# RWKV preparation: shifted mixing read from PSUM, three banks for the in-projection, low parts of its weights on the vector engine

## The chip, the cores and the metric

The kernel runs on one core of a Trainium2 chip. The time is the device time of the whole program in microseconds (us); before the change it is 1434.59, the median of 3 runs (1434.33 to 1435.47).

The engines are named as the profile names them: PE multiplies matrices (PEld loads its stationary operand), DVE is the vector engine, ACT the scalar engine, POOL the GpSimd engine, SP only issues DMAs. Each takes its instructions in the order in which the compiler's scheduler has put them. SBUF is the on-chip memory. PSUM, where PE writes its results, has eight banks of 128 partitions x 512 float32 values.

## The reference, cut to what matters

Two layers over 256 latent and 256 context tokens of width 1024. The first mixes tokens with RWKV-7 heads and differential attention side by side, the second is a Mamba-2 mixer; each ends with an MLP. The change lies in the preparation of the RWKV heads:

```python
def centred_shift(p):
    prev = jnp.pad(p[:, :-1], ((0, 0), (1, 0), (0, 0)))
    nxt = jnp.pad(p[:, 1:], ((0, 0), (0, 1), (0, 0)))
    return 0.5 * (prev + nxt)

# rwkv_prepare: p is the first 1792 columns of h @ w_in, for latent and context tokens
    p = p + (centred_shift(p) - p) * mu
    r, k, v, wd, ad, gd = jnp.split(p, ...)
    kkf = hd(k * k_k)
    kk = kkf * lax.rsqrt(jnp.sum(kkf * kkf, axis=-1, keepdims=True) + 1e-12)
```

So every column of the projection becomes `(1 - mu) * p[t] + (mu / 2) * (p[t-1] + p[t+1])`, with zero beyond the ends of each of the two sequences.

## The kernel before, in words

Activations lie transposed, 128 channels on the partitions, 512 tokens (256 latent, 256 context) along the free dimension. To keep float32 accuracy with the faster matmul type, a matrix is split in a high part (rounded) and a low part (the rest), and a product is three matmuls: high by high, high by low, low by high.

The in-projection runs over tiles of 128 columns. `unit` (line 359) is one half of such a tile: four blocks of 128 rows, twelve matmuls 128x512 into one bank; `in_half` (line 367) calls it for both halves. The weights of a unit come through `w_ahead` (line 349): a DMA on SP's queue into `rw`, ACT's copy into the high part `rh` (line 355), and a subtraction into the low part `rl` (line 356) on the engine that `enqueue` (line 370) gave, POOL by default. All three rings have three buffers, and each unit that starts asks for the weights two units on. Fourteen tiles (28 units) belong to the RWKV preparation, twelve more to attention, whose projection follows and partly overlaps; the same rings later serve the out-projection.

`units` (line 660) is the backbone of the preparation: it projects a tile, and `shiftmix` (line 537) evacuates and mixes it. ACT copies the bank into a padded tile `pad` and writes the bank scaled by 1 - mu to `smq`; DVE adds the padded tile's two shifted views (`sms`) and combines both with mu / 2 into the result (`krv`, or once each `wda` and `sg`). After each step `units` runs small pieces of work from the list `after` (line 690): per pair of heads `kk_norm` (line 553: squares, a small matmul into `kkps`, a reciprocal square root of eleven DVE operations on eight columns, tiles `nw_x`, `nw_t`, `nw_y`, then a matmul `kkb` that spreads it and a DVE multiply `kk`), `v_tok`, and `stream` for context and latent tokens (line 582: decay matmuls `zp`, `ap`; DVE, ACT and POOL work on `lt`, `cs`, `e`; products AR and BK; matmuls `Lps`; a small matmul `bp` and the store `bond` of `bo` on SP's queue). One step of `ada`, the modulation vectors of the layer (matmuls `adaps`), is run per unit as well. After the last stream, the 64x64 triangular inverses (`rwkv_T`, line 441) start with 62 dependent DVE operations each, and attention's projections and softmax run beside them.

PSUM in this part: pool `mm` two banks (in-projection), `g` three (`kkps`, `kkb`, `vp`, `bp`, `gt`), `ch` three. The three stay open to the end of attention. The order on each engine is not that of the program text alone: a scheduler at compile time orders by priority and by when it estimates operands to be ready.

Of the kernel before, what the change touches and what calls it, by code (L numbers as in the profile page):

```python
# [7 lines left out]
F32 = mybir.dt.float32  # L8
F32R = mybir.dt.float32r
I32 = mybir.dt.int32  # L10
AF = mybir.ActivationFunctionType
# [4 lines left out]
ADD, SUB, MUL, MIN, MAX = ALU.add, ALU.subtract, ALU.mult, ALU.min, ALU.max  # L16

D = 1024
T = 256
NT = 512  # L20
# [31 lines left out]
def build(ctx: ExitStack, tc, xT, cT, pk_d, ct_d, ca_d, cs_d, lora_d, gup_d, cb_d, ada_w, adaT, w_in, w_out, w1, w2,  # L52
          s_in, s_dt, s_out, out, dbg=None, stop=None):
    nc = tc.nc
    act, dve, pool, pe = nc.scalar, nc.vector, nc.gpsimd, nc.tensor

    def dump(name, ap):
        if dbg is not None and name in dbg:
            nc.sync.dma_start(out=dbg[name], in_=ap)
# [4 lines left out]
    cm = ExitStack()  # L64
    mid = cm.enter_context(tc.tile_pool(name="mid", bufs=1, side="right"))
    dram = ctx.enter_context(tc.tile_pool(name="dram", bufs=1, space=DRAM))
    def ps_pools(stack, *bufs):
        for n, b in zip(("mm", "g", "ch"), bufs):
            PS[n] = stack.enter_context(tc.tile_pool(name=f"ps_{n}", bufs=b, space=PSUM, reuse_waits="tile"))

    PS = {}
# [5 lines left out]
    def tt(o, a, b, op):  # L77
        dve.tensor_tensor(o, a, b, op)  # L78

    def ts(o, a, s1, op0, s2=None, op1=None):  # L80
        if op1 is None:
            dve.tensor_scalar(o, a, s1, None, op0)
        else:
            dve.tensor_scalar(o, a, s1, s2, op0, op1)

    def stt(o, a, s, b, op0, op1):
        dve.scalar_tensor_tensor(o, a, s, b, op0, op1)  # L87

    def actf(o, i, f, scale=1.0, bias=0.0, **kw):
        act.activation(out=o, in_=i, func=f, scale=scale, bias=bias, **kw)  # L90

    def psm(shape, name="mm"):
        return PS["mm"].tile(shape, F32, name=name, tag="mm")

    def psg(shape, name="g"):
        return PS["g"].tile(shape, F32, name=name, tag="g")
# [52 lines left out]
    def kview(w):  # L149
        return w.rearrange("(p j) n -> p j n", j=8)  # L150
# [175 lines left out]
    E2 = [slice(0, 64), slice(64, 128)]  # L326
    Q = lambda d, b: slice(64 * d + 32 * b, 64 * d + 32 * b + 32)
    with ExitStack() as c1:
        ps_pools(c1, 2, 3, 3)
        reg = c1.enter_context(tc.tile_pool(name="reg", bufs=1))  # L330

        cr = reg.tile([128, NCT - 256], F32, name="cr")
# [8 lines left out]
        wv = kview(w_in)  # L341
# [25 lines left out]
        def in_half(ps, i):  # L367
            unit(ps, hh, hl, 4 * i, i == 0, i == 1)

        def enqueue(v, cols, ks=(0, 4), engs=(pool,)):  # L370
            todo.extend((v, c, k, engs[i % len(engs)]) for i, c in enumerate(cols) for k in ks)

        for k in (0, 4):
            enqueue(wv, [1536, 512], (k,))
        enqueue(wv, [0, 1024])
        for hp in range(1, 4):
            enqueue(wv, [512 + 128 * hp, 128 * hp, 1024 + 128 * hp])
        enqueue(wv, [1664])
        for hd in range(4):
            enqueue(wv, [1792 + 512 * i + 128 * hd for i in range(3)])  # L380

# [4 lines left out]
        with tc.tile_pool(name="x0", bufs=1) as xp:  # L386
# [3 lines left out]
            i = iter(range(16))  # L390
# [114 lines left out]
        with tc.tile_pool(name="prep", bufs=1) as pp:  # L505
            def ring(name, shape, bufs):
                return pp.tile(shape, F32, name=name, tag=name, bufs=bufs)
# [7 lines left out]
            mu1, muh = sm[:, 32:46], sm[:, 46:60]  # L515
# [7 lines left out]
            ts(rkh, PV("rk"), 0.5, MUL)  # L523
            wda = pp.tile([128, NT], F32, name="wda")
            sg = pp.tile([128, NT], F32, name="sg")
            pads = [pp.tile([128, 2, T + 2], F32, name=f"pad{i}") for i in range(2)]
            for p_ in pads:
                pool.memset(p_[:, :, 0:1], 0.0)
                pool.memset(p_[:, :, T + 1:T + 2], 0.0)
            e1s = [pp.tile([128, 2, 4, 66], F32, name=f"e1{i}") for i in range(2)]  # L530
            for e in e1s:
                e = e.rearrange("p d c t -> p (d c) t")
# [1 line left out]
                pool.memset(e[:, :, 65:66], 1.0)  # L534
            rot = [0]

            def shiftmix(n, o, ps=None):
                if ps is None:
                    ps = psm([128, NT], "inps")
                    in_half(ps, 0)  # L540
                    yield
                    in_half(ps, 1)
                pad = pads[rot[0] % 2]
                rot[0] += 1
                p3 = lambda a: a.rearrange("p (s t) -> p s t", s=2)
                actf(pad[:, :, 1:T + 1], p3(ps), AF.Copy)
                q = ring("smq", [128, NT], 2)
                s = ring("sms", [128, NT], 2)
                actf(q, ps, AF.Identity, scale=mu1[:, n:n + 1])
                tt(p3(s), pad[:, :, 0:T], pad[:, :, 2:T + 2], ADD)  # L550
                stt(o, s, muh[:, n:n + 1], q, MUL, ADD)

            def kk_norm(hp, k):

# [104 lines left out]

            def units():  # L660

                p2 = [psm([128, NT], "inps") for _ in range(2)]
                for i in range(2):
                    for ps in p2:
                        in_half(ps, i)
                    yield
                yield from shiftmix(12, wda, p2.pop(0))
                actf(wda[0:64], wda[0:64], AF.Tanh)
                yield
                for hp in range(4):  # L670
                    krvs.append([])
                    for sec in (1, 0, 2):
                        krvs[hp].append(ring("krv", [128, NT], 6))
                        yield from shiftmix(4 * sec + hp, krvs[hp][-1], p2.pop() if p2 else None)
                        yield
                yield from shiftmix(13, sg)
                actf(sg, sg, AF.Tanh, scale=0.5)
                ts(sg, sg, 0.5, MUL, 0.5, ADD)
                yield
                for _ in range(2):  # L680
                    early.append(psm([128, NT], "inps"))
                    for i in range(2):
                        in_half(early[-1], i)
                        yield
# [17 lines left out]
            with ExitStack():  # L702
                for u, _ in enumerate(units()):
                    for f in after.get(u, ()):
                        f()
                    if u > 1:
                        next(A, None)
                run((A, 1))
            dump("wda", wda)
            dump("sg", sg)  # L710

        at = c1.enter_context(tc.tile_pool(name="at", bufs=1, reuse_waits="tile"))

# [394 lines left out]


    ps_pools(ctx, 3, 2, 3)  # L1110
    wpool = ctx.enter_context(tc.tile_pool(name="w", bufs=2, reuse_waits="tile"))
    def gemm_first(pss, wts, rh, rl, n, lat_norm=None):
# [147 lines left out]
    with ExitStack() as c1:  # L1260
# [14 lines left out]
        def t1k(shape, name, **kw):  # L1275
            return sp.tile(shape, F32, name=name, tag="t1k", bufs=4)
# [5 lines left out]
        ps = done.pop(0)  # L1282
# [7 lines left out]
        f = [t1k([128, 4, 64], f"sf{i}") for i in range(4)]  # L1290
        tt(dts, pt, PV("dtb").unsqueeze(1).to_broadcast([128, 4, 64]), ADD)
        e, r, s2, p_ = f
# [18 lines left out]
        cp = psg([128, 4, 64], "cps")  # L1311
# [376 lines left out]
```

## Time and profile before

| | |
|---|---|
| median of 3 runs | 1434.59 us |
| the profiled execution | 1438.96 us, of which the span from first to last instruction is 1437.2 |
| busy share of the span | PE 94%, DVE 74%, ACT 44%, POOL 21% |
| granted PE clock, mean | 0.974 of full |

How to read it: "busy" is the time in which an engine had an instruction running. A row of a group names the line of the kernel, the engine and the operation, the output tile, an arrow and the inputs, the shape and the count; then busy us, mean ns of one, and the idle time just before them with what ended it. A row in order of time begins with start and duration in us; a bracket at its end is the idle time before it and who released it. The line can be that of a helper (L75 is every matmul, L78 every `tensor_tensor`, L84 and L82 `tensor_scalar`, L87 `scalar_tensor_tensor`, L90 every activation), so tiles tell more than lines. The chain of waits that ended last was followed back as far as 472 us only, so for the preparation, which lies before that, the stretches and the waits are read instead.

### The profile page before, as it was taken

The page shows a single profiled execution, that of the slowest core. Times are in us where ns is not written, and L with a number is a line of the kernel's source. Part 1 is how long each engine was busy: PE and PEld are TensorE (multiplying, and loading weights), DVE is VectorE, ACT ScalarE, POOL GpSimd, SP SyncE. Part 2 cuts the span into 40 slices and gives each one's busy share as a digit, 9 for nine tenths or more (in the row PEclk, how much of TensorE's full clock was granted, in tenths as well). Part 3 has the DMA queues.
Part 4 walks back from the last instruction along what each step waited for, and adds up shares of the span by engine and source line. Part 5 has one row for each costly group of instructions (what it writes and reads, how often), then busy time and mean ns, then how long its engine had stood idle before and what let it go on. Part 6 is the DMA issues. An engine that isn't in the chain of part 4 may idle for free.

```text
span 1437.2 us, 25996 instructions
## 1 busy us (share of the span) xinstructions
PE 1351.4 (94%) x10026; PEld 1139.1 (79%) x10026; DVE 1059.2 (74%) x2217; ACT 638.8 (44%) x1200; POOL 302.5 (21%) x228
## 2 busy tenths in 40 slices
PE   5899998899998799999999999999999989999997
PEld 2566666677877788888888897888888879999997
DVE  3778869864778898987667567697778784766665
ACT  2544444454543444224232243665555533455543
POOL 0355443111004300000000001233333335311110
PEclk9999999899999899999999999999999999999999
DMA  9455565234143556656667433655444323566653
GB/s 343 146 186 183 180 181 139 56 89 170 44 143 95 155 156 188 185 179 210 211 196 214 146 107 95 164 168 140 132 117 133 103 88 93 155 188 183 191 178 102
DMA packets 311324, 220.42 MB, mean 153 GB/s; under 512 B 30176, under 2 KB 279840, under 8 KB 310048
## 3 DMA queue, kind: packets, MB, share of 16 engines
q1 hardware_dynamic: 306080, 210.36, 49.2%
q10 hardware_dynamic: 3968, 4.20, 0.9%
q0 software_dynamic: 1152, 4.19, 0.8%
q8 instruction: 79, 1.29, 0.4%
q14 instruction: 45, 0.37, 0.1%
HBM read 205.54 MB, written 13.17 MB: 152 GB/s over the span
## 4 chain that ended last, share of the span: by engine, by line
PE 60%; DVE 5%; ACT 1%; issue 1%; DVEq 0%; ACTq 0%
PE m L75 37%; PE xsp L75 5%; PE zp L75 3%; PE so L75 3%; PE bm L75 3%; PE first L75 1%; PE cm L75 1%; PE ssdy L75 1%; PE hst L75 1%; PE xtp L1434 1%; DVE cva L87 0%; PE gn L75 0%; PE gnb L75 0%; PE hlat L75 0%; PE nps L75 0%
## 5 line engine op out<-in xcount | busy, mean ns | idle before, releaser
L90 ACT ACTIVATE wh<-wraw 128x1024 fp32r<-128x1024 f32 x197 | 208.2, 1058 | 367.8 <-PE m L75 258.0
L146 POOL TENSOR_TENSOR wl<-wraw,wh 128x1024 fp32r<-128x1024 f32 x55 | 133.0, 2423 | 614.2 <-ACT wh L90 614.2
L75 PE MATMUL m<-hid,wh 128*128 128x256 f32 (+1 forms) x1152 | 257.2, 319 | 0.5 <-DVE hid L78 0.5
L146 DVE TENSOR_TENSOR wl<-wraw,wh 128x1024 fp32r<-128x1024 f32 x142 | 173.7, 1223 | 44.5 <-ACT wh L90 44.2
L75 PEld LDWEIGHTS m<-hid,wh 128*128 128x128 f32 x1152 | 190.8, 189 | 17.0 <-DVE hid L78 0.7
L75 PE MATMUL m<-hid,wl 128*128 128x256 f32 (+1 forms) x576 | 183.4, 319 | 0.0
L356 POOL TENSOR_TENSOR rl<-rw,rh 128x512 fp32r<-128x512 f32 x73 | 99.3, 1366 | 261.2 <-ACT rh L90 252.8
L75 PEld LDWEIGHTS m<-hid,wl 128*128 128x128 f32 x576 | 108.9, 189 | 7.7
L75 PE MATMUL m<-hh,wh 128*128 128x512 f32 (+1 forms) x264 | 103.3, 394 | 1.6 <-ACT wh L90 1.6
L75 PE MATMUL m<-hh,wl 128*128 128x512 f32 (+1 forms) x264 | 103.1, 393 | 1.7 <-POOL wl L146 1.7
L75 PE MATMUL m<-hl,wh 128*128 128x512 f32 (+1 forms) x264 | 103.1, 393 | 0.0
L246 DVE CUSTOM_DVE_ANT_0 arow<-arow,cb 128x512 f32<-128x512 f32 x112 | 76.0, 688 | 28.3 <-DMA arow<-in_adaT_dram 26.8
L75 PE MATMUL inps<-hh,rh 128*128 128x512 f32 x208 | 89.5, 433 | 3.4 <-ACT hh L90 3.4
L90 ACT ACTIVATE rh<-rw 128x512 fp32r<-128x512 f32 x73 | 45.6, 628 | 100.0 <-PE inps L75 41.2
L75 PE MATMUL inps<-hl,rh 128*128 128x512 f32 x208 | 85.2, 411 | 1.2 <-DVE hl L78 1.2
L75 PE MATMUL inps<-hh,rl 128*128 128x512 f32 x208 | 85.3, 411 | 0.0
L75 PE MATMUL m<-uh,wh 128*128 128x258 f32 x256 | 73.5, 288 | 2.3 <-ACT uh L90 2.3
L75 PE MATMUL m<-uh,wl 128*128 128x258 f32 x256 | 73.4, 287 | 0.0
L75 PE MATMUL m<-ul,wh 128*128 128x258 f32 x256 | 73.3, 286 | 0.0
L75 PEld LDWEIGHTS m<-hh,wl 128*128 128x128 f32 x264 | 50.5, 192 | 13.3 <-POOL wl L146 2.0
L75 PEld LDWEIGHTS m<-hh,wh 128*128 128x128 f32 x264 | 50.8, 193 | 12.8 <-ACT wh L90 1.6
L75 PEld LDWEIGHTS m<-hl,wh 128*128 128x128 f32 x264 | 50.6, 192 | 11.2
(691 smaller groups left out, 3360.4 us busy)
## 6 DMA issues: line engine op xcount, KB each, us to landing
wraw<-in_w_dram SPq DMA_DIRECT2D x133, 512.0 KB, 3.9
arow<-in_adaT_dram SPq DMA_DIRECT2D x112, 256.0 KB, 3.3
wraw<-in_s_in_dram SPq DMA_DIRECT2D x48, 512.0 KB, 4.3
rw<-in_w_in_dram SPq DMA_DIRECT2D x52, 256.0 KB, 3.3
arow<-in_ada_w_dram SPq DMA_DIRECT2D x48, 256.0 KB, 3.7
araw<-in_ada_w_dram SPq DMA_DIRECT2D x16, 512.0 KB, 10.2
csb<-csd SPq DMA_DIRECT2D x8, 1024.0 KB, 6.4
wraw<-in_s_out_dram SPq DMA_DIRECT2D x16, 512.0 KB, 3.9
```

The source lines that it names most:

```text
L75: pe.matmul(o, lhsT=l, rhs=r, start=start, stop=stop)
L90: act.activation(out=o, in_=i, func=f, scale=scale, bias=bias, **kw)
L146: eng.tensor_tensor(l, raw, h.bitcast(F32), SUB)
L246: dve.tensor_tensor_reduce(r if s == ns - 1 else junk, r, cb[:, s, i * W:i * W + W], 0.5, 0.0, MUL, ADD, sums[:, s, j, i:i + 1])
L356: eng.tensor_tensor(l, r, h.bitcast(F32), SUB)
L1434: pe.transpose(tp[:, q, i * 128:i * 128 + 128], xs[:, i, t0:t0 + 128], ident)
```

## The change

Three things are changed, all in the first layer's mixing part.

The mixing no longer uses a padded copy. ACT writes the bank scaled by 1 - mu straight into the result; two fused DVE operations (255 elements in each of the two sequences) then add mu / 2 times the bank, shifted by one token to the right and to the left, onto it in place. The bank is held until the second of these has read it.

PSUM is divided anew while the preparation lasts: `bank` takes every third tile from a new pool `x` of one bank and the others from `mm`, `g` has two banks, `ch` three. After it these pools are closed, and `g` and `ch` are opened with three banks each. The two attention tiles that are projected early still come from `mm`.

The low parts of the 28 RWKV units are formed on DVE; those of attention and of the out-projection stay on POOL.

```diff
-    def ps_pools(stack, *bufs):
-        for n, b in zip(("mm", "g", "ch"), bufs):
+    def ps_pools(stack, *bufs, names=("mm", "g", "ch")):
+        for n, b in zip(names, bufs):
...
-        ps_pools(c1, 2, 3, 3)
+        ps_pools(c1, 2)
+        cp = ExitStack()
+        ps_pools(cp, 1, 2, 3, names=("x", "g", "ch"))
...
         for k in (0, 4):
-            enqueue(wv, [1536, 512], (k,))
-        enqueue(wv, [0, 1024])
+            enqueue(wv, [1536, 512], (k,), (dve,))
+        enqueue(wv, [0, 1024], (0, 4), (dve,))
         for hp in range(1, 4):
-            enqueue(wv, [512 + 128 * hp, 128 * hp, 1024 + 128 * hp])
-        enqueue(wv, [1664])
+            enqueue(wv, [512 + 128 * hp, 128 * hp, 1024 + 128 * hp], (0, 4), (dve,))
+        enqueue(wv, [1664], (0, 4), (dve,))
...
-            pads = [pp.tile([128, 2, T + 2], F32, name=f"pad{i}") for i in range(2)]
-            for p_ in pads:
-                pool.memset(p_[:, :, 0:1], 0.0)
-                pool.memset(p_[:, :, T + 1:T + 2], 0.0)
...
+            def bank():
+
+                rot[0] += 1
+                return PS["x"].tile([128, NT], F32, name="inps", tag="x") if rot[0] % 3 == 0 else psm([128, NT], "inps")
+
             def shiftmix(n, o, ps=None):
                 if ps is None:
-                    ps = psm([128, NT], "inps")
+                    ps = bank()
...
-                pad = pads[rot[0] % 2]
-                rot[0] += 1
                 p3 = lambda a: a.rearrange("p (s t) -> p s t", s=2)
-                actf(pad[:, :, 1:T + 1], p3(ps), AF.Copy)
-                q = ring("smq", [128, NT], 2)
-                s = ring("sms", [128, NT], 2)
-                actf(q, ps, AF.Identity, scale=mu1[:, n:n + 1])
-                tt(p3(s), pad[:, :, 0:T], pad[:, :, 2:T + 2], ADD)
-                stt(o, s, muh[:, n:n + 1], q, MUL, ADD)
+                actf(o, ps, AF.Identity, scale=mu1[:, n:n + 1])
+                for i, j in ((slice(0, T - 1), slice(1, T)), (slice(1, T), slice(0, T - 1))):
+                    stt(p3(o)[:, :, j], p3(ps)[:, :, i], muh[:, n:n + 1], p3(o)[:, :, j], MUL, ADD)
...
-                p2 = [psm([128, NT], "inps") for _ in range(2)]
+                p2 = [bank() for _ in range(2)]
...
+        cp.close()
+        ps_pools(c1, 3, 3, names=("g", "ch"))
```

## Prediction

> **What bounds the kernel now.** I read the page first, then the busy time by stretches, then the waits and groups of the stretch that the change touches, and last the order of time around each wait of the matrix engine in it.
>
> ```profile
> span 1437.2 us, 25996 instructions
> ...
> 40.00:55.00 15.00, 11.96 (x39) 9.19 (x40) 14.93 (x36) 9.97 (x20) 5.51 (x12) 0.77 0.24 68
> ...
> 55.00:195.00 140.00, 133.99 (x1113) 90.53 (x1113) 108.77 (x167) 65.36 (x145) 68.54 (x61) 1.00 0.59 183
> ...
> 195.00:206.00 11.00, 10.76 (x44) 7.56 (x42) 3.03 (x8) 3.39 (x7) 6.59 (x8) 1.00 0.62 198
> 206.00:242.00 36.00, 32.88 (x176) 24.17 (x177) 34.70 (x95) 12.49 (x31) 14.09 (x13) 0.95 0.55 154
> ```
>
> The columns of a stretch are its length, then busy us of PE, PEld, DVE, ACT and POOL, then the granted PE clock and the DMA share. The preparation runs from 55 to 195. PE is busy 133.99 of 140 us there, at full clock: only 6.01 us are free, so no relief of DVE, ACT or POOL can shorten these 140 us by more than 6. DVE is at 78%, with no room to fall far behind. From 206 on it is the other way round: DVE works 34.70 of 36 us.
>
> Where the 6 us lie, and the one wait that matters for the risk (total, times, longest):
>
> ```profile
> PE kkb L75 <- DVE nw_y L87: 5.1, 4, 1.8
> ...
> ACT rh L90 <- DMA rw<-in_w_in_dram: 10.0, 3, 6.6
> ```
>
> PE stands 5.1 us, in four waits, before the matmul that spreads the norm of k (tile kkb). It waits for a chain of eleven tiny DVE operations, the reciprocal square root. Nothing else holds PE for more than a fraction of a us. What makes that chain late is seen in order of time (start, duration):
>
> ```profile
> 73.81 1.26 DVE L84 TENSOR_SCALAR nw_y<-nw_x 128x8 int32<-128x8 int32 x1
> 75.11 0.17 DVE L78 TENSOR_TENSOR nw_t<-nw_y,nw_x 128x8 f32<-128x8 f32 x1
> ...
> 76.32 1.27 DVE L78 TENSOR_TENSOR nw_t<-nw_y,nw_x 128x8 f32<-128x8 f32 x1
> ...
> 73.56 1.48 POOL L356 TENSOR_TENSOR rl<-rw,rh 128x512 fp32r<-128x512 f32 x1
> 76.31 1.26 POOL L356 TENSOR_TENSOR rl<-rw,rh 128x512 fp32r<-128x512 f32 x1 [1.26 <-DMA rw<-in_w_in_dram]
> ...
> 78.05 1.09 PE L75 MATMUL kkb<-ct,nw_y 128*64 128x128 f32 x16 [1.76 <-DVE nw_y L87]
> ...
> 108.59 1.29 POOL L356 TENSOR_TENSOR rl<-rw,rh 128x512 fp32r<-128x512 f32 x1
> ...
> 108.69 1.22 DVE L78 TENSOR_TENSOR nw_t<-nw_t,nw_y 128x8 f32<-128x8 f32 x1
> ...
> 111.58 1.09 PE L75 MATMUL kkb<-ct,nw_y 128*64 128x128 f32 x16 [1.44 <-DVE nw_y L87]
> ...
> 142.26 1.29 POOL L356 TENSOR_TENSOR rl<-rw,rh 128x512 fp32r<-128x512 f32 x1 [0.35 <-ACT rh L90]
> ...
> 142.38 1.19 DVE L87 SCALAR_TENSOR_TENSOR nw_y<-nw_t,nw_y 128x8 f32<-128x8 f32 x1
> ...
> 145.04 1.09 PE L75 MATMUL kkb<-ct,nw_y 128*64 128x128 f32 x16 [0.75 <-DVE nw_y L87]
> ...
> 174.33 0.47 DVE L84 TENSOR_SCALAR nw_y<-nw_x 128x8 int32<-128x8 int32 x1
> ...
> 174.73 1.28 POOL L356 TENSOR_TENSOR rl<-rw,rh 128x512 fp32r<-128x512 f32 x1
> ...
> 174.83 1.20 DVE L78 TENSOR_TENSOR nw_t<-nw_y,nw_x 128x8 f32<-128x8 f32 x1
> ...
> 177.91 1.09 PE L75 MATMUL kkb<-ct,nw_y 128*64 128x128 f32 x16 [1.16 <-DVE nw_y L87]
> ```
>
> An operation of eight columns takes 0.17 us, the integer one 0.47. Five of them take 1.2 to 1.3. At 73.56 and 76.31 POOL is inside the subtraction that forms a weight's low part, and the DVE operation that starts then ends just after POOL does (73.56 + 1.48 = 75.04 against 73.81 + 1.26 = 75.07; 77.57 against 77.59). So DVE stands still while POOL reads. The excess is 0.79 + 1.10 in the first chain and 1.05, 1.02 and 1.03 in the others, 5.0 us, against PE waits of 1.76 + 1.44 + 0.75 + 1.16 = 5.1. The waits are the POOL excess, nearly one to one.
>
> **The change part by part.** Groups of the preparation (count | busy us, mean ns | idle before):
>
> ```profile
> L87 DVE SCALAR_TENSOR_TENSOR krv<-sms,sm,smq 128x512 f32<-128x512 f32 x12 | 17.7, 1476 | 1.9 <-ACT smq L90 0.7
> L78 DVE TENSOR_TENSOR sms<-pad 128x512 f32<-128x512 f32 x14 | 16.3, 1162 | 10.4 <-ACT pad L90 10.4
> ...
> L78 DVE TENSOR_TENSOR lt<-lt,krv 128x512 f32<-128x512 f32 x8 | 5.5, 693 | 0.3
> ...
> L87 DVE SCALAR_TENSOR_TENSOR kk<-krv,sm,kkb 128x512 f32<-128x512 f32 x4 | 3.0, 748 | 4.8 <-PE kkb L75 4.8
> ...
> L87 DVE SCALAR_TENSOR_TENSOR wda<-sms,sm,smq 128x512 f32<-128x512 f32 x1 | 1.6, 1587 | 0.1
> L87 DVE SCALAR_TENSOR_TENSOR sg<-sms,sm,smq 128x512 f32<-128x512 f32 x1 | 0.8, 752 | 0.1
> ...
> L90 ACT ACTIVATE pad<-inps 128x512 f32<-128x512 f32 x14 | 8.1, 581 | 1.4 <-PE inps L75 1.4
> ...
> L356 POOL TENSOR_TENSOR rl<-rw,rh 128x512 fp32r<-128x512 f32 x26 | 36.4, 1408 | 34.3 <-ACT rh L90 32.9 <-DMA rw<-in_w_in_dram 1.3
> ```
>
> *Mixing.* Fourteen times, an ACT copy (8.1 us in all) and two DVE operations go: 16.3 + 17.7 + 1.6 + 0.8 = 36.4 us of DVE. In come 28 fused operations that read the bank, 510 elements each. The nearest row is kk, which reads a bank too: 0.748, so 28 x 0.748 = 20.9. The same operation on SBUF alone took 0.752 when undisturbed (sg), so I take no surcharge for the bank. [...]
>
> Do the new operations stand still behind POOL? One DVE operation that reads a bank fell wholly inside a POOL pair:
>
> ```profile
> 97.12 0.41 DVE L78 TENSOR_TENSOR bo<-krv,bp 128x256 f32<-128x256 f32 x1
> ...
> 95.23 3.09 POOL L356 TENSOR_TENSOR rl<-rw,rh 128x512 fp32r<-128x512 f32 x2
> ```
>
> It was not held. I take the same for the new ones. This part is off PE's path (ACT is at 47%, and no wait of a matmul names a mixing): worth 15.5 us of DVE and 8.1 of ACT, nothing of the time by itself.
>
> *Low parts on DVE.* 28 of these subtractions leave POOL. Of the table's 26 the last three belong to attention's columns and stay, so 23 of the moved ones lie in the 140 us and five before. On DVE the nearest row is a 512-wide subtraction's equal, 0.693: 23 x 0.693 = 15.9 us. DVE: 108.8 - 36.4 + 20.9 + 15.9 = 109.2, before the other operations that POOL now holds are let go, 5.0 us of them in the norm chains alone. So about 104 us, 74%: DVE does not become the bound. The gain is the 5.1 us of PE waits, less what a subtraction costs when it falls into a norm chain itself, 0.69 each. POOL's fell into all four. Bounds: five of them stay in (5 x 0.69 = 3.5, gain 1.6), or none, and the small PE waits go too (6.0). I take one in two chains: 5.1 - 1.4 = 3.7.
>
> *Start.* The first weights' low parts meet the splitting of the normed input:
>
> ```profile
> 40.34 0.42 DVE L78 TENSOR_TENSOR hl<-nap,hh 128x256 fp32r<-128x256 f32 x1
> ...
> 42.22 1.49 DVE L78 TENSOR_TENSOR hl<-nap,hh 128x256 fp32r<-128x256 f32 x1
> ...
> 40.88 2.55 POOL L356 TENSOR_TENSOR rl<-rw,rh 128x512 fp32r<-128x512 f32 x2 [1.26 <-ACT rh L90]
> ...
> 43.76 0.80 PE L75 MATMUL inps<-hl,rh 128*128 128x512 f32 x1 [1.17 <-DVE hl L78]
> ```
>
> POOL ends at 43.43, hl after it, and PE waited 1.17. Without POOL that hl is about 1.1 earlier; with both subtractions queued ahead of it on DVE, 1.4 later. So a gain between 1.2 and a loss of 1.4. I take 0.6 gained: one subtraction ahead, 1.17 - 0.69, and a little of the 0.77 clock.
>
> *Banks.* The in-projection goes from two banks to three, the small products from three to two until the preparation ends. Holding a bank until DVE has read it twice adds two reads, 1.5 us, to its life; fourteen tiles in 140 us come some 10 apart, so a third bank gives 10 more. The other side: two banks must do for five small tiles per head pair, one every 7 us. I cost both at nothing; if a small tile did wait, it would be for one DVE read, 0.41 (bo) to 0.75 (kk). The pools opened anew afterwards get banks whose last readers are done. The memsets of the pads and SBUF moved: nothing.
>
> *Sum.* 3.7 + 0.6 = 4.3 us off the profiled 1438.96 (span 1437.2 and 1.8 around it), so 1434.7. That execution lies 4.4 above the median of the runs, 1434.59; off the median it is **1430.3**. I let it pass whole to the end. What follows at 206 is DVE's triangular inverse,
>
> ```profile
> 206.44 0.18 DVE L462 TENSOR_TENSOR tb<-Lp,Z 128x31 f32<-128x31 f32 x1
> ```
>
> whose input is the preparation's last product, so it moves along.
>
> **The rivals.** *A: the gain is spent (about 1434.0).* Subtractions sit in every norm chain (gain 1.6) and the first ones cost 1.0 at the start; or the inverse keeps its place at 206.44, since it is DVE-bound from there and 195 to 206 has no PE idle to give. For it: the POOL subtractions overlap all four chains now. Against: every step up to the inverse hangs on PE's progress. 1434.6 - 0.6 = 1434.0.
>
> *B: DVE stands behind weights (1440.3).* DVE's queue is in order, and each subtraction now waits in it for ACT's high part, which waits for the load:
>
> ```profile
> 111.56 0.40 SPq L354 DMA_DIRECT2D rw<-in_w_in_dram  x1
> ...
> 114.58 0.63 ACT L90 ACTIVATE rh<-rw 128x512 fp32r<-128x512 f32 x1 [6.55 <-DMA rw<-in_w_in_dram]
> ```
>
> Today only ACT and POOL stand there, while DVE does kk and its products. Queued behind the subtraction would be kk, then AR and BK, which PE's next small matmuls need. If DVE loses the 10.0 us of the wait row and all of it reaches PE, the time is 1434.6 + 10.0 - 4.3 = 1440.3. It decides from the point where more than 4.3 of the 10 reach PE. Against it: DVE has 31 us idle in the 140 to take it up. [...]
>
> *C: all of it and more (1425.0).* No subtraction in a chain (6.0), the start's 1.2, and 2.4 from the inverse starting sooner because DVE's work in front of it is shorter. Against: DVE is nearly idle from 195 to 206 already.
>
> **How the numbers follow.** Forecast 0.48, A 0.22, B 0.17, C 0.13. The range reaches from just below C to 1438.0, which leaves out the worse half of B. A measurement of this kernel can tell about 0.2%, 2.9 us. Faster by more than that: C and most of the forecast, whose low end (gain 1.6 to 2.9) is no change: 0.13 + 0.44 = 0.57. Same: A, that low end and the mild part of B, 0.28. Slower: 0.15.
>
> **What would show it.** Right: the four kkb waits sum to under 2 us, norm operations back at 0.17, PE in the preparation over 98% busy, DVE near 104 us in a stretch about 4 shorter, mixing operations at 0.75. Wrong: a PE wait on Lps, kkps or bp released by DVE; DVE idle released by ACT rh for several us; mixing operations far over 0.75; an inverse that starts no earlier than 206.

## The result, and the profile after

The changed kernel takes **1425.29 us** (median of 6 runs, 1425.04 to 1426.88) against 1434.69 for the kernel before (median of 6), a ratio of 0.9933 with a 95% interval of 0.9917 to 0.9949: 9.4 us faster. The forecast was 4.3 us faster. The profiled execution took 1426.16 us, its span 1424.4. It began its first in-projection 2.6 us earlier than the profiled one of before, of which some 1.9 us were there ahead of anything that was changed (the input x alone landed 1.6 us earlier), so the two profiles differ by 12.8 us where the medians differ by 9.4.

The same stretches as before (length, busy us of PE, PEld, DVE, ACT and POOL, granted PE clock, DMA share, GB/s):

```profile
40.00:55.00 15.00, 14.25 (x57) 10.76 (x60) 14.16 (x44) 9.68 (x19) 0.22 (x4) 0.90 0.45 146
55.00:195.00 140.00, 137.96 (x1135) 95.60 (x1128) 99.93 (x186) 59.00 (x131) 42.32 (x44) 1.00 0.62 187
195.00:206.00 11.00, 10.52 (x81) 7.41 (x80) 10.42 (x27) 4.10 (x8) 6.30 (x7) 1.00 0.83 240
```

In the preparation PE is busy 137.96 of 140 us where it was 133.99, DVE 99.93 where it was 108.77. From 195 to 206 DVE now works 10.42 of 11 us instead of 3.03: the inverse has already begun, 9.4 us earlier than before, the 1.9 us of the beginning included:

```profile
197.01 0.18 DVE L464 TENSOR_TENSOR tb<-Lp,Z 128x31 f32<-128x31 f32 x1
```

Of the waits of PE in the preparation the longest is still that for the norm:

```profile
PE kkb L75 <- DVE nw_y L87: 1.4, 3, 0.9
```

It was 5.1 us in four. The groups of DVE in the preparation (count, busy us, mean ns, idle before):

```profile
L358 DVE TENSOR_TENSOR rl<-rw,rh 128x512 fp32r<-128x512 f32 x22 | 18.9, 859 | 4.4 <-ACT rh L90 2.6 <-PE bp L75 1.6
L87 DVE SCALAR_TENSOR_TENSOR krv<-inps,sm,krv 128x510 f32<-128x510 f32 x23 | 17.1, 743 | 0.5 <-ACT krv L90 0.3
...
L87 DVE SCALAR_TENSOR_TENSOR nw_y<-nw_t,nw_y 128x8 f32<-128x8 f32 x12 | 3.5, 290 | 0.3
...
L78 DVE TENSOR_TENSOR nw_t<-nw_y,nw_x 128x8 f32<-128x8 f32 x12 | 1.9, 162 | 0.2
```

The norm operations are back at 0.16 us but for a few, and the mixing operations take 0.743. What stands inside a norm chain now is seen in its second occurrence:

```profile
95.85 0.95 PE L75 MATMUL kkps<-cr,smq 128*128 128x2 f32 x8
...
96.83 0.17 DVE L84 TENSOR_SCALAR nw_x<-kkps 128x8 f32<-128x8 f32 x1 [0.53 <-PE kkps L75]
97.03 0.76 DVE L84 TENSOR_SCALAR nw_y<-nw_x 128x8 int32<-128x8 int32 x1
97.70 1.30 DVE L358 TENSOR_TENSOR rl<-rw,rh 128x512 fp32r<-128x512 f32 x1
98.93 0.73 DVE L87 SCALAR_TENSOR_TENSOR krv<-inps,sm,krv 128x510 f32<-128x510 f32 x1
...
99.70 0.75 DVE L87 SCALAR_TENSOR_TENSOR krv<-inps,sm,krv 128x510 f32<-128x510 f32 x1
...
100.55 1.01 DVE L87 SCALAR_TENSOR_TENSOR bsum<-bsum,sm,krv 128x256 f32<-128x256 f32 x1
...
102.89 0.69 DVE L358 TENSOR_TENSOR rl<-rw,rh 128x512 fp32r<-128x512 f32 x1
...
104.02 0.17 DVE L87 SCALAR_TENSOR_TENSOR nw_y<-nw_t,nw_y 128x8 f32<-128x8 f32 x1
```

The chain is not shorter than before. From the start of kkps to the end of the last nw_y it takes 104.19 - 95.85 = 8.34 us; before it took 5.98 (105.54 to 111.52). Two subtractions, a whole mixing and a bsum lie in it. Yet PE waits less. Why that is so is what the experiments had to find.

### The profile page after: what moved, and what is told of

Read it like the earlier page. It is cut to its first block, busy times and chain, and to the rows that moved or that the text cites. A ratio compares the mean times of both kernels' runs of the same rounds, so it can differ in the third digit from the quotient of the medians.

```text
span 1424.4 us, 25962 instructions
## 1 busy us (share of the span) xinstructions
PE 1348.7 (95%) x10026; PEld 1139.4 (80%) x10026; DVE 1046.4 (73%) x2245; ACT 632.3 (44%) x1186; POOL 264.5 (19%) x196
## 4 chain that ended last, share of the span: by engine, by line
PE 61%; DVE 5%; ACT 1%; issue 1%; DVEq 0%; ACTq 0%
PE m L75 38%; PE xsp L75 5%; PE zp L75 3%; PE bm L75 3%; PE so L75 3%; PE first L75 1%; PE cm L75 1%; PE ssdy L75 1%; PE hst L75 1%; PE xtp L1434 1%; PE nps L75 0%; DVE cva L87 0%; PE gn L75 0%; PE hlat L75 0%; PE gnb L75 0%
## 5 line engine op out<-in xcount | busy, mean ns | idle before, releaser
L358 POOL TENSOR_TENSOR rl<-rw,rh 128x512 fp32r<-128x512 f32 x45 | 59.9, 1333 | 187.2 <-ACT rh L90 177.2
L75 PE MATMUL inps<-hl,rh 128*128 128x512 f32 x208 | 85.7, 413 | 0.2 <-DVE hl L78 0.2
L75 PEld LDWEIGHTS m<-hh,wl 128*128 128x128 f32 x264 | 50.5, 192 | 11.5
```

Source lines behind the costliest of these rows:

```text
L75: pe.matmul(o, lhsT=l, rhs=r, start=start, stop=stop)
L358: eng.tensor_tensor(l, r, h.bitcast(F32), SUB)
```

## The experiments

Theory P, from the prediction: the time comes from POOL's reads, which hold DVE in the norm chain; the rest of the change is worth nothing. The rivals: the mixing has a share, by DVE's relief; or the three banks; or the start. Each kernel below was timed in five rounds beside the kernel before (medians 1435.45 to 1435.58). "Prep" is the time from the first in-projection product to the first tb of the inverse, "inverse" from there to the start of the last Z, both from the profiled execution, with PE's waits for kkb. These stages show where time goes, but they don't add up to the medians: a profiled execution lies up to 5.6 us from its kernel's median (e2's 5.6 below), and what follows the inverse differs between them by up to 9 us (1138 to 1147).

| kernel | median us | ratio to before, 95% | kkb waits | prep | inverse |
|---|---|---|---|---|---|
| before | 1434.69 | | 5.1 | 164.6 | 84.2 |
| the change | 1425.29 | 0.9933, 0.9917 to 0.9949 | 1.4 | 157.7 | 82.9 |
| e1 low parts only | 1429.59 | 0.9952, 0.9935 to 0.9969 | 1.8 | 159.0 | 85.9 |
| e2 mixing only | 1444.72 | 1.0059, 1.0038 to 1.0079 | 11.9 | 172.8 | 82.5 |
| e3 mixing and low parts | 1425.61 | 0.9922, 0.9900 to 0.9944 | 0.7 | 156.8 | 82.5 |
| e4 mixing and banks | 1444.67 | 1.0057, 1.0037 to 1.0076 | 11.5 | 174.0 | 82.6 |
| e5 before, low parts by ACT | 1427.93 | 0.9952, 0.9938 to 0.9967 | none | 156.6 | 83.6 |
| e6 change, low parts by ACT | 1431.20 | 0.9966, 0.9949 to 0.9983 | 3.7 | 161.6 | 82.8 |
| e7 before, first four on DVE | 1435.35 | 0.9994, 0.9980 to 1.0008 | 4.0 | 164.8 | 86.2 |
| e8 change, first four on POOL | 1429.09 | 0.9963, 0.9951 to 0.9975 | 0.8 | 158.8 | 82.1 |
| e9 before, kkb later | 1434.67 | 0.9989, 0.9976 to 1.0002 | none | 164.7 | 84.6 |
| e10 mixing only, kkb later | 1431.47 | 0.9964, 0.9947 to 0.9982 | none | 162.7 | 85.7 |
| e11 change, kkb later | 1428.64 | 0.9946, 0.9928 to 0.9964 | none | 158.2 | 84.6 |
| e12 change, attention's too | 1414.71 | 0.9851, 0.9832 to 0.9870 | 1.4 | 157.6 | 76.1 |

### The parts alone

e1, on the kernel before (and so for every `enqueue` of the preparation):

```diff
-            enqueue(wv, [1536, 512], (k,))
+            enqueue(wv, [1536, 512], (k,), (dve,))
```

> Only the low parts move from POOL to DVE; mixing and banks as before. Theory P (the gain is DVE let go from POOL's reads, in the norm chains and at the start): nearly the whole gain, 6 to 9 us under the kernel before (1434.7), so 1426 to 1429, and kkb waits under 2 us. Theory M (the gain is the shorter mixing): DVE gets 16 us more work and nothing less, so no gain or a loss, 1434 to 1438. Theory B (the third bank): about 1434.7.

e2, the new `shiftmix` with two banks, low parts on POOL; e3, the change without the third bank; e4, the change with the low parts left on POOL:

```diff
-                return PS["x"].tile([128, NT], F32, name="inps", tag="x") if rot[0] % 3 == 0 else psm([128, NT], "inps")
+                return psm([128, NT], "inps")
...
-            enqueue(wv, [1536, 512], (k,), (dve,))
+            enqueue(wv, [1536, 512], (k,))
```

> Only the mixing is new (read from the bank, two banks of the in-projection as before, low parts on POOL). P: the norm chains are still held, kkb waits stay near 5 us, gain 0 to 2, so 1433 to 1435. M: 5 to 9 us gained, 1426 to 1430. B: the longer hold of two banks shows as waits of the first matmul of a tile, and the time is 1435 or more.

> The change without its third bank (mixing new, low parts on DVE, banks 2, 3, 3 as before). P and M: as the whole change, 1425.3 within 1.5. B: PE waits for banks, at least 3 us slower than the whole change, 1428 or more.

> The change with its low parts left on POOL. P: nearly the kernel before, 1432 to 1435, kkb waits near 5 us again, and the start as before. M: nearly the whole change, 1425 to 1428. B: between, with most of the gain there.

The banks do nothing: e3 is at the change's time, e4 at e2's. Rival B's time for e2, 1435 or more, came without its reason: one first matmul of a tile waits 1.15 us there, released by ACT's krv, and in e4, where no such wait is left, the time is the same. The low parts alone give 6.0 us; e1's time lies 0.6 us above P's range. The mixing alone, which I had put at nothing, *costs* 9.1 us, and beside the low parts it gives 4.0 to 4.3. The same edit has opposite signs, so its worth is not in its own work. In e2 the second norm chain reads, on DVE, POOL and PE:

```profile
107.59 0.66 DVE L78 TENSOR_TENSOR nw_t<-nw_y,nw_x 128x8 f32<-128x8 f32 x1
108.28 1.22 DVE L78 TENSOR_TENSOR nw_t<-nw_t,nw_y 128x8 f32<-128x8 f32 x1
...
109.82 0.74 DVE L87 SCALAR_TENSOR_TENSOR krv<-inps,sm,krv 128x510 f32<-128x510 f32 x1
...
111.45 1.00 DVE L87 SCALAR_TENSOR_TENSOR bsum<-bsum,sm,krv 128x256 f32<-128x256 f32 x1
112.38 0.64 DVE L78 TENSOR_TENSOR nw_t<-nw_y,nw_x 128x8 f32<-128x8 f32 x1
113.06 1.18 DVE L78 TENSOR_TENSOR nw_t<-nw_t,nw_y 128x8 f32<-128x8 f32 x1
...
108.17 1.30 POOL L356 TENSOR_TENSOR rl<-rw,rh 128x512 fp32r<-128x512 f32 x1
111.49 1.50 POOL L633 TENSOR_TENSOR AR<-krv,e 128x256 f32<-128x256 f32 x2 [2.01 <-DVE nw_y L87]
112.96 1.25 POOL L356 TENSOR_TENSOR rl<-rw,rh 128x512 fp32r<-128x512 f32 x1
...
105.62 0.95 PE L75 MATMUL kkps<-cr,smq 128*128 128x2 f32 x8
...
110.45 0.59 PE L75 MATMUL bp<-bsum,cr 128*128 128x256 f32 x2
114.50 1.98 PE L75 MATMUL kkb<-ct,nw_y 128*64 128x128 f32 x16 [3.45 <-DVE nw_y L87]
```

Two things are to be seen. Tiny operations end just after POOL's subtractions do (109.50 against 108.17 + 1.30 = 109.47). And DVE's queue now has the mixing of the next tile and a bsum between the norm steps, where the old one ran its mixing ahead of them. It has one ACT step less ahead of it, and, as I read it, the scheduler found room for it in the chain's gaps. kkb stands right behind bp in PE's queue and waits.

### Is it POOL's silence, or the order?

e5, on the kernel before, and e6, on the change, give the 28 low parts to ACT as a copy of the weight, which leaves the subtraction out:

```diff
-                eng.tensor_tensor(l, r, h.bitcast(F32), SUB)
+                if eng is act:
+                    actf(l, r, AF.Copy)
+                else:
+                    eng.tensor_tensor(l, r, h.bitcast(F32), SUB)
```

> The kernel before, with the 28 low parts of the in-projection weights written by ACT as a plain copy of the weight. The low part itself is not computed, so the product is not the reference's; what is tested is the time when POOL no longer reads SBUF there and DVE gets no work for it. Theory P (POOL's reads hold DVE's norm chain): the four waits for kkb fall from 5.1 us to under 2, the norm operations return to 0.17 us, and the time is that of the low parts on DVE (1429.6) or up to 2 us less, since no subtraction sits in a chain; ACT's 23 further copies of 0.63 us (14.5 us on 65 of 140) may give some of it back, to 1431. Rival Q (what helped was another order on DVE's and SP's queues, not POOL's silence): waits stay near 5 us and the time near 1435.6.

> The changed kernel, with the 28 low parts written by ACT as a plain copy (not computed, so the product is not the reference's): the new mixing with POOL silent and DVE free of the subtractions. Theory P (the mixing loses only because its shorter chain comes to lie under three of POOL's stretches): waits for kkb under 2 us and 1423 to 1427, like the whole change. Rival M (the mixing itself delays the norm chain, and DVE's subtractions made up for it by moving the loads): waits for kkb 8 us or more and about 1440.

e5 confirms P for the kernel before: with POOL's subtractions gone and DVE given nothing, no wait for kkb is left and prep falls by 8.0 us. The groups of DVE in its preparation:

```profile
L78 DVE TENSOR_TENSOR sms<-pad 128x512 f32<-128x512 f32 x13 | 10.6, 816 | 10.4 <-ACT pad L90 10.4
L87 DVE SCALAR_TENSOR_TENSOR krv<-sms,sm,smq 128x512 f32<-128x512 f32 x12 | 10.2, 850 | 1.3
...
L78 DVE TENSOR_TENSOR nw_t<-nw_y,nw_x 128x8 f32<-128x8 f32 x12 | 2.0, 167 | 0.4
```

The old mixing's operations fall from 1162 and 1476 ns to 816 and 850, the norm's from 383 to 167.

e6 missed its forecast, under 2 us of waits and 1423 to 1427. With POOL's subtractions gone the new mixing still makes PE wait 3.7 us for kkb, and its prep is 5.0 us longer than e5's. Rival M's 8 us of waits and 1440 did not come either. So P alone doesn't explain the mixing's loss; the order in the chain does the rest. For the second chain I read two times from each profile: from the start of kkps to the end of the last nw_y (ready), and from the start of kkps to where kkb stands, its own wait taken off (due):

| kernel | ready | due | wait |
|---|---|---|---|
| before | 5.98 | 4.60 | 1.44 |
| e5 | 4.13 | 4.51 | none |
| e1 | 5.65 | 5.07 | 0.63 |
| e2 | 8.82 | 5.43 | 3.45 |
| e6 | 7.11 | 5.42 | 1.84 |
| the change | 8.34 | 7.60 | 0.88 |
| e3 | 7.73 | 7.62 | 0.16 |

The wait is ready less due, but for the 0.1 us or so of the hand-over. The mixing makes the chain ready about 3 us later (e5 to e6) but due only 0.9 later. Due is the same with POOL's subtractions as without them (before and e5, e2 and e6): the order doesn't reckon with the hold. The subtractions on DVE it does reckon with, and they put kkb another 2.2 us later in PE's queue (e6 to the change). That is why the mixing loses without them and not with them. Theory W: what counts is how late the chain is against kkb's place.

### Moving the place of kkb alone

e9 on the kernel before, e10 on e2, e11 on the change:

```diff
-                for u, f in ((2, step(S1)), (3, step(K)), (4, step(K)), (5, step(S0)), (6, step(S1)),
+                for u, f in ((2, step(S1)), (3, step(K)), (5, step(K)), (5, step(S0)), (6, step(S1)),
```

> The kernel before, with the second half of the norm of k (norm chain, spreading product kkb, kk) handed out one unit later, so that kkb stands 7 to 10 matmuls of 0.233 us later in the matrix engine's queue and POOL still forms the low parts. Theory W (what the hold costs is only that kkb comes due before the held chain ends): the four waits for kkb fall from 5.1 us to under 1, about 4 to 5 us faster, 1431. Rival H (POOL's hold on DVE's other operations, sms, krv, bsum, costs the time too, and the wait shows up at the next product that DVE feeds): under 2 us faster, with new waits for Lps or bp.

> The new mixing alone (low parts on POOL, two banks) with the same shift of kkb, here 13 places of the queue, some 3.0 us, later. Theory W: the mixing alone lost 9 us because its plan put kkb right behind bp while POOL held the chain for 3 us longer than planned; with the place moved the waits fall from 11.9 us to under 2 and the time from 1444.7 to 1431 to 1434. Rival H: the wait moves on to Lps, and the time stays over 1440.

> The changed kernel with the same shift, 7 places later, some 1.6 us. Theory W: only the 1.4 us of waits for kkb that are left can go: 1424 to 1425.3, no difference that can be measured. Rival: kk, and with it AR, BK and Lps, comes later, and the next product waits: 1427 or more.

For the mixing W holds: e10's chain is no faster than e2's (ready 8.89), but it is due at 9.41, no wait is left, and 13 of the 1444.72 us go without POOL or DVE being relieved of anything. In the profiles prep falls by 10.1 us, of which the inverse takes 3.2 back. The second chain of e10:

```profile
101.48 0.95 PE L75 MATMUL kkps<-cr,smq 128*128 128x2 f32 x8
...
110.20 0.17 DVE L87 SCALAR_TENSOR_TENSOR nw_y<-nw_t,nw_y 128x8 f32<-128x8 f32 x1
...
110.89 1.09 PE L75 MATMUL kkb<-ct,nw_y 128*64 128x128 f32 x16
```

For the kernel before W's number fails and H's holds: the waits for kkb go, and the time hardly moves, because another wait takes their place (e9, waits of PE from 40 to 215):

```profile
PE Lps L75 <- DVE AR L87: 3.5, 4, 1.2
```

Why is seen in the order of time behind e9's second kkb:

```profile
111.23 1.09 PE L75 MATMUL kkb<-ct,nw_y 128*64 128x128 f32 x16
...
112.30 1.38 DVE L78 TENSOR_TENSOR sms<-pad 128x512 f32<-128x512 f32 x1 [1.50 <-ACT pad L90]
113.60 0.73 DVE L87 SCALAR_TENSOR_TENSOR kk<-krv,sm,kkb 128x512 f32<-128x512 f32 x1
...
111.86 1.27 POOL L356 TENSOR_TENSOR rl<-rw,rh 128x512 fp32r<-128x512 f32 x1 [2.70 <-ACT rh L90]
```

kk now stands behind the next tile's sms, which waits for ACT and is then held by POOL (1.38 us, where e5's took 0.82 on the mean); kk, AR and Lps all come later. In e10 the operation in that place is one of the new mixing: at 112.06 it takes 0.75 us beside a POOL subtraction from 111.52 to 112.79, so it is not held, and Lps waits 0.4 us in all. e11 shows no gain over the change, as W said. Its median, 1428.64, lies in the rival's range, but Lps waits only 0.3 us there and the two intervals overlap, so a small loss is neither shown nor excluded.

### The start

e7 moves the first four subtractions alone on the kernel before, e8 takes them back on the change:

```diff
         for k in (0, 4):
-            enqueue(wv, [1536, 512], (k,))
+            enqueue(wv, [1536, 512], (k,), (dve,))
```

> The kernel before, with only the first four low parts (first tile pair) on DVE. Theory S (the start is worth more than the 0.6 us predicted: hl's wait 1.2, ACT's wait for POOL 0.7, and the half-speed stretch of PE after it 1.5): 2 to 3 us faster, 1433 to 1433.5, with PE at full clock from about 44 us and the waits for kkb as before, near 5. Rival (the start is worth what the prediction said, 0.6, because what PE gains there it loses at the next wait): 1435, ratio 0.9996.

> The changed kernel with the first four low parts back on POOL. Theory S: 2 to 3 us slower than the whole change, 1427.5 to 1428.5, PE at half clock until 49 us, waits for kkb still under 2. Rival (start worth 0.6): 1426.

The change begins its in-projection so:

```profile
39.27 0.87 PE L75 MATMUL inps<-hh,rh 128*128 128x512 f32 x2 [2.70 <-ACT hh L90]
40.31 0.79 PE L75 MATMUL inps<-hl,rh 128*128 128x512 f32 x1 [0.17 <-DVE hl L78]
...
42.60 0.63 PE L75 MATMUL inps<-hh,rh 128*128 128x512 f32 x1
43.03 0.45 PE L75 MATMUL inps<-hl,rh 128*128 128x512 f32 x1
43.32 0.39 PE L75 MATMUL inps<-hh,rl 128*128 128x512 f32 x1
```

The wait for hh is 0.73 us shorter (3.43 before), that for hl 1.0, and the matmuls go from 0.43 us apart to 0.23 some 4 us after the first one; before it took 7.5 us. On the kernel before, e7, all this is lost again at once, and the time is the rival's:

```profile
50.90 2.66 DVE L82 TENSOR_SCALAR sm<-pk 128x14 f32<-128x14 f32 x5
...
53.62 0.68 DVE L356 TENSOR_TENSOR rl<-rw,rh 128x512 fp32r<-128x512 f32 x1
...
50.81 2.66 POOL L356 TENSOR_TENSOR rl<-rw,rh 128x512 fp32r<-128x512 f32 x2
...
54.35 0.80 PE L75 MATMUL inps<-hh,rl 128*128 128x512 f32 x1 [2.66 <-DVE rl L356]
```

The fourth subtraction is queued behind five small operations, which take 2.66 us while POOL forms the next units' low parts; in the kernel before five such took 0.45. Moving some of them only puts DVE's share behind POOL's. On the change taking them back costs 1429.09 - 1425.29 = 3.8 us by the medians; the two intervals of the ratio lie just apart. The profiles show 1.1 us of it in prep (157.7 to 158.8) and a shorter inverse, so where the rest lies is not shown.

### Attention's low parts too

```diff
-            enqueue(wv, [1792 + 512 * i + 128 * hd for i in range(3)])
+            enqueue(wv, [1792 + 512 * i + 128 * hd for i in range(3)], (0, 4), (dve,))
```

> The changed kernel with the low parts of attention's 24 weight blocks on DVE as well. 14 of POOL's 24 lie between 197 and 280 us, where DVE's inverse is the bound. Theory P (a read of POOL costs DVE more than the subtraction costs it): at a hold of 0.7 to 1.3 us against 0.69 us each, 0 to 8 us faster, 1417 to 1425, with operations tb and Z of 192 and more columns back near their shortest. Rival L (in a stretch that DVE bounds, 14 x 0.69 = 9.7 us more DVE work costs most of itself, since POOL's reads hold only part of the inverse): 1428 to 1432.

At 1414.71 us this is better than both kernels, 20.7 us under before and 10.6 under the change, and 2.3 under P's range. The inverse shortens from 82.9 to 76.1 us although DVE does 16 subtractions within it. Another 3.6 us lie between the end of the last Z and the first product of the out-projection (113.0 to 109.4); what shortens that part was not tried. DVE's groups from 197 to 280, first of the change, then of e12:

```profile
L464 DVE TENSOR_TENSOR tb<-Lp,Z 128x87 f32<-128x87 f32 x4 | 3.5, 886 | 0.1
L464 DVE TENSOR_TENSOR tb<-Lp,Z 128x156 f32<-128x156 f32 x4 | 3.3, 820 | 0.0
L464 DVE TENSOR_TENSOR tb<-Lp,Z 128x240 f32<-128x240 f32 x4 | 2.7, 672 | 0.0
```

```profile
L358 DVE TENSOR_TENSOR rl<-rw,rh 128x512 fp32r<-128x512 f32 x17 | 11.7, 687 | 2.0 <-ACT rh L90 2.0
...
L464 DVE TENSOR_TENSOR tb<-Lp,Z 128x240 f32<-128x240 f32 x4 | 1.6, 399 | 0.0
...
L464 DVE TENSOR_TENSOR tb<-Lp,Z 128x156 f32<-128x156 f32 x4 | 1.3, 318 | 0.1
...
L464 DVE TENSOR_TENSOR tb<-Lp,Z 128x87 f32<-128x87 f32 x4 | 1.0, 248 | 0.1
```

Rival L had counted the work at 9.7 us and was right on that (11.7 for 17), wrong on the price of the alternative. The PE clock in that stretch is granted at 0.99 instead of 0.90.

## Why the prediction was right, and where not

**What bounds it: right.** PE bounded the preparation. Prep became 6.8 us shorter, start and all, against 6 us free in the stretch, and PE is at 98.5% there.

**The waits are POOL's hold: right.** With the subtractions off POOL and nothing put on DVE (e5) they vanish, and so do the 383 ns means. "Nearly one to one" holds for the sum alone: chain by chain the excess was 1.89, 1.05, 1.02 and 1.03 us against waits of 1.76, 1.44, 0.75 and 1.16. A chain that is ready before kkb is due, as e5's second by 0.38 us, takes some hold without a wait, and in the second chain POOL's AR holds one operation more (0.61 us at 108.04, where it ends at 108.65 and POOL's AR at 108.63). Nor are the waits themselves the price: moving kkb alone (e9) removes all 5.1 us of them and gains 0.8, because the held operations then make Lps wait 3.5; what had to go is the hold.

**Mixing, "nothing of the time by itself": wrong, and the step that failed.** Its durations were right: 0.743 for 0.748 us, and 0.747 in e2 amid POOL's subtractions, against 0.752 for the same operation on SBUF alone, so in these rows reading a bank shows no surcharge and no hold. But I priced the operations by their time and looked for a matmul that waits for a mixing. In the changed kernel none does. The operations went into another chain's gaps and made that later by some 3 us (e6), and kkb's place in PE's queue decided whether this shows. It cost 9.1 us alone and brought 4.0 to 4.3 beside the low parts. That the term put at nothing came out on the good side was luck: nothing in the prediction reckoned with the place of kkb. Of this gain 1.3 to 2.2 us lie in prep (159.0 to 157.7 and 156.8) and some 3 in the inverse (85.9 to 82.9 and 82.5), which stays open below.

**Low parts on DVE, 3.7 us: right in kind, too small.** With the start's 0.6 the sum was 4.3; e1 measured 6.0, with an interval that begins at 4.5. The subtractions took 859 ns, not 693, since POOL's remaining BK, BKs, bsum and AR still hold some: six of the 22 start while one of these runs and took 1.13 to 1.73, the others 0.68 or 0.69; DVE came to 99.9 us in the 140, not 104. I expected one subtraction in each of two chains; in the changed kernel the second chain alone has two, but a subtraction in a chain that moves kkb too is not a wait. e1's waits for kkb fell by 3.3 us, about what I said; the rest would be the start and what I had called "the other operations that POOL now holds", which no run measured apart.

**Start, 0.6 us: not refuted alone, too small in company.** e7 gives 0.2 us, with an interval on both sides of nothing; e8 gives 3.8 by the medians, of which prep shows 1.1.

**Banks, nothing: right** (e3, e4).

**"Pass whole to the end": not quite.** The inverse takes 82.1 to 86.2 us in the kernels before e12, with the same DVE operations. e12 shows that POOL's subtractions are worth 6.8 us there, so a shift in when they fall is a likely cause; it was not tried by itself, and stays open.

**The rivals.** B's hole did open, but small: DVE stood 2.6 us before subtractions for ACT's high part, and no wait of PE came of it. Rival C's time, 1425.0, is what was measured, not for its reasons throughout: the norm waits were not all gone, and what it took from the inverse comes from the inverse itself. A's fear, that subtractions sit in the chains, came true without its price.

## What to carry to other kernels

Where the reads of one engine hold another, as POOL's subtractions held DVE here (0.17 us became up to 1.27), they are charged to the busy one: before counting an engine's free time, line up its slow operations with the other's by end time. An operation that is off the critical path can still lengthen a chain of tiny operations into whose gaps the scheduler puts it; compare when the chain is ready with where its consumer stands in its queue, and price two edits together if one of them moves that place. When a hold is found, remove it wherever it reaches, not in the one stage: here the stretch that DVE bounds gave 6.8 us more, as much as the preparation that was looked at.

## What the runs showed of the hardware

DVE's operations of eight columns with two SBUF operands took 0.17 us alone and up to 1.27 beside a POOL subtraction (75.11 and 76.32 in the kernel before); operations that take one operand from a bank kept 0.41 (97.12 in the kernel before) and 0.75 (112.06 in e10) beside one. The traces also show operations with one tile operand held: the five small `sm` ones of e7 took 2.66 us beside POOL, five such 0.45 in the kernel before. What decides whether an operation is held was not tried. In the inverse the hold cost more than the work: 82.9 us against 76.1 with 16 operations added.

Behind some of its longer waits PE ran at about half speed. In e2 the 3.45 us wait was followed by a kkb group of 1.98 us instead of 1.09. In e4 the groups read:

```profile
113.20 1.97 PE L75 MATMUL kkb<-ct,nw_y 128*64 128x128 f32 x16 [3.53 <-DVE nw_y L87]
...
150.16 1.98 PE L75 MATMUL kkb<-ct,nw_y 128*64 128x128 f32 x16 [2.90 <-DVE nw_y L87]
...
185.28 1.09 PE L75 MATMUL kkb<-ct,nw_y 128*64 128x128 f32 x16 [2.89 <-DVE nw_y L87]
```

Waits of 2.90 and 2.89 had different ends, so the length of the wait alone doesn't decide in these rows. Shorter waits were followed by it too: behind e4's first, 2.17 us, the kkb group took 1.58 us, and the in-projection matmuls from 80.24 to 81.10 started 0.43 us apart, where 0.23 is usual; behind e2's first, 2.84, the group took 1.09 and the matmuls from 81.07 to 83.20 started 0.43 apart; behind e2's third, 2.81, the group took 1.09 and the matmuls started 0.23 apart. What sets the half speed off is not shown.
